# Where the maxima return in an attention quarter, the place of the bias in every second quarter, and the products that release banks first

## The chip, the cores and the metric

The kernel runs on one core of one Trainium2 chip. The metric is the device time of one execution in microseconds (us). Before the change three runs took 632.68, 632.74 and 633.77 us (median 632.74 us). Engine names are those of the profile: PE (matrix products; PEld is its weight load), DVE (vector engine), ACT (scalar engine), POOL and SP (here mostly the issue of DMAs).

## The reference

The program is one layer of a hybrid block: 1024 latent tokens of width 1024 (a grid of 16 rows by 64 columns), 256 context tokens, one input projection, neighbourhood attention with 8 heads of 64 beside a gated short convolution, and one output projection, all in float32. The change lies in the attention:

```python
def neighbourhood_attention(q, k, v, kc, vc, rpb):
    ...
    s_lat = jnp.einsum('biqhd,birkhd->bhiqrk', q_rot, k_rows,
                       preferred_element_type=jnp.float32) * scale + bias
    s_lat = jnp.where(col_valid[:, None, :], s_lat, -jnp.inf)
    s_ctx = jnp.einsum('biqhd,blhd->bhiql', q_plain, kc,
                       preferred_element_type=jnp.float32) * scale
    ...
    p = jax.nn.softmax(s, axis=-1).astype(v.dtype)
    ...
    o = (jnp.einsum('bhiqrk,birkhd->biqhd', p_lat, v_rows)
         + jnp.einsum('bhiql,blhd->biqhd', p_ctx, vc))
```

The convolution branch appears as `bg * centred_short_conv(cg * u) * silu(zc)`; its last product reads a bank of PSUM (the memory into which PE writes its products).

## The kernel before

Every float32 operand is split into a high and a low part, and a product is three products (high by high, high by low, low by high). In the first 262 us the tokens are normalised and projected and keys, queries and values are stored; then comes the attention; from 539 us on the output projection.

The attention is a loop of 35 **quarters**, `quarter(n)`, four to a head. Quarter `n` does parts of several quarters' work: it makes the scores of quarter `n` and the context scores of `n + 1`; it makes the exponentials of `e = n - 2`; and it multiplies the weights of `o = n - 3` by the values. During a quarter PE also runs `TICKS[n]` **ticks** (`next(fill)`), six products each of 128x512, of the projections that attention does not need yet: the attention gate `z`, then for three conv groups the columns u, cg, z and bg. Each such unit (`unit`) fills two banks of PSUM, one half after the other, under the name `pu`; there are two such banks, so the first half of the next unit can start only when the first half of the last one has been read.

While attention runs, the order on PE, ACT, DVE and POOL is that in which the code calls them (`strict`), and each engine waits at the instruction at its head. The order in quarter `n`:

1. `maxima(e)`: two transposes on PE of the running maxima `mx` into a bank `pmx`, and on DVE the reduction `rm` over them. It returns `back`: two transposes on PE of the spread `rm` into the same bank, and the copy `mg` on ACT.
2. On DVE the low part `pll` that is left over from the quarter before (`lat_rest`).
3. `ctx_out(o)`, where `o` is odd: six products `po` of the context's weights `phc`, `plc` and the values.
4. `do_dves(3)`: waiting work of DVE, at most three pieces besides the `soon` queue. Pieces of the `slow` queue with a third entry are those that release a bank `pu`: `times` of the columns bg, the product `cv<-pu,cv`. Then a step of `gating`, if there is one.
5. Where `o` is odd and live (`early`; these are the even quarters 4 to 34): `back()`.
6. `scores`: four products into `pss`. `ctx_scores`: four products into `pc` and their copy `sc` on ACT.
7. Where not `early`: `back()`.
8. For `e`: on DVE the difference `sc<-sc,mg`, on ACT two exponentials (`phc` and `sc`); on DVE the difference `sb<-sb,mg`, on ACT two exponentials (`phl` and `sb`).
9. One tick, then `lat_out(o)`: products `po` of `phl`, `pll`.
10. On DVE the bias, `sb<-pss,bt` (one instruction or two), then the running maxima: `mx<-pc,sc` and two `mx<-mx,sb`. The next quarter's `maxima` needs the last of them.
11. On DVE `plc<-sc,phc`. The remaining ticks; `finish`, which copies a finished bank to `ob`; `do_acts`, waiting work of ACT.

So in an odd quarter PE makes the transposes back after the context's four scores, and in an even one between the context's six products and the scores. In every quarter the bias stands behind the two differences on DVE.

Of the kernel before, what the change touches and what calls it, by code (L numbers as in the profile page):

```python
# [14 lines left out]
ALU = mybir.AluOpType  # L15
# [10 lines left out]
NB = 8  # L26
# [13 lines left out]
def body(tc, es, x, ctxt, w_ada, b_ada, w_in, q_g, k_g, rpbr, w_out, vecs, cst, out):  # L40
# [21 lines left out]
    pe, act, dve, pool = every = [ordered(e) for e in (nc.tensor, nc.scalar, nc.vector, nc.gpsimd)]  # L62
# [258 lines left out]
    def do_acts():  # L321
        for c in soon + (slow if not any(c[1] and c[1].__name__ == "product" for c in soon) else []):
            if c[0]:
                c[0]()
                c[0] = None

    def do_dves(most=99):
        while most > 0 and slow and slow[0][2] is not None and not slow[0][0]:
            slow.pop(0)[1]()
            most -= 1  # L330
        for queue in chores:
            while queue and not queue[0][0] and (queue is soon or most > 0 and not soon):
                on_dve = queue.pop(0)[1]
                if on_dve:
                    on_dve()
                    most -= 1
# [205 lines left out]
    def tr():  # L542
        return ps0.tile([P, 512], F32, name="tr", tag="tr", bufs=2)
# [48 lines left out]
    pv = tr()  # L592
# [243 lines left out]
    for m in range(1, 4):  # L836
        k, new, last = 2 * m, m < 3, m == 3
# [169 lines left out]
    class head:  # L1007
# [28 lines left out]
            self.bt = bmp.tile([P, 3, 384], F32, name="bt", tag="bt", bufs=2)  # L1036
            sp.dma_start(self.bt[:].rearrange("p v n -> p (v n)")[:, :1128], t4_d[self.h])

        def ctx_scores(self, g):
            pc = psm.tile([P, 2, 256], F32, name="pc", tag="C", bufs=2)  # L1040
            q = self.q[:, 1, g * 256:(g + 1) * 256]
            for i in range(2):
                for l in range(2):
                    pe.matmul(pc[:, i], self.kc[:, l, i * P:(i + 1) * P], q,
                              start=(i == 0 and l == 0), stop=(i == 1 and l == 1), skip_group_check=True)
            sc = ap.tile([P, 2, 256], F32, name="sc", tag="sc", bufs=4)
            act.copy(sc, pc)
            self.cps[g] = sc, pc
# [12 lines left out]
            m = seen(mx[:], j)  # L1061
            dve.tensor_tensor(m, m, cells(sb, j), ALU.max)

        def pv(self, bank, cols, j, ph, pl, last):
            first = bank not in self.po
            if first:
                self.po[bank] = psm.tile([P, 512], F32, name="po", tag="O", bufs=2)
            o_ = cols(self.po[bank][0:HD + 1])
            vh, vl = self.v[:, 0, j], self.v[:, 1, j]
            pe.matmul(o_, vh, ph, start=first, stop=False, skip_group_check=True)  # L1070
            pe.matmul(o_, vl, ph, start=False, stop=False, skip_group_check=True)
            pe.matmul(o_, vh, pl, start=False, stop=last, skip_group_check=True)

# [17 lines left out]
            del self.cps[g]  # L1091
            return lambda: dve.tensor_tensor(pl, sc, ph.bitcast(F32), ALU.subtract)

        def ctx_out(self, g):
            if g % 2:
                ph, pl = self.cx
                for i in range(2):
                    self.pv(g // 2, lambda o: o, NB + i, ph[:, i], pl[:, i], False)

        def finish(self, bank):  # L1100

# [5 lines left out]
    def pair_of(n):  # L1107

        h, g = divmod(n, 4)
        return [(a, heads[h], 2 * g + a) for a in range(2)] if 0 <= h < NH else []  # L1110

    def both(v, n, part=slice(0, 31)):

        lo, hi = span(2 * (n % 4))
        return v[:, :, part.start * 12:min(part.stop, hi - lo) * 12]

    def maxima_of(n):

        lo, hi = span(2 * (n % 4))
        v = mg[:]  # L1120
        return bass.AP(v.tensor, v.offset + lo * 16, [list(v.ap)[0], [4, 2], [16, hi - lo], [1, 12]])

    def turned(n):

        g = n % 4
        return [b for b, there in (((2 * g + 2) % NB, n + 1 < 4 * NH), (2 * g + 1, n >= 0)) if there][::-1 if g < 3 else 1]

    def maxima(e):

        blocks = turned(e) if e < 4 * NH else []  # L1130
        nb = len(blocks)
        if not blocks:
            return None
        pm = psm.tile([P, 512], F32, name="pmx", tag="C", bufs=2)
        for i, b in enumerate(blocks):
            pe.transpose(pm[:, i * P:(i + 1) * P], mx[:, b * P:(b + 1) * P], ident)
        rm = ap.tile([P, 2], F32, name="rm", tag="rm", bufs=8)
        dve.tensor_reduce(rm[:, :nb], pm[:, :nb * P].rearrange("p (i k) -> p i k", i=nb), AX.X, ALU.max)

        def back():  # L1140
            for i in range(nb):
                pe.transpose(pm[:, 256 + i * P:256 + (i + 1) * P], rm[:, i:i + 1].broadcast_to([P, P]), ident)
            v, step = mg[:, blocks[0] * P:], (blocks[-1] - blocks[0]) * P or P
            act.copy(bass.AP(v.tensor, v.offset, [list(v.ap)[0], [step, nb], [1, P]]),
                     pm[:, 256:256 + nb * P].rearrange("p (i k) -> p i k", i=nb))
        return back

    def quarter(n):

        live = lambda m: 0 <= m < 4 * NH
        ticks = TICKS[n]
        e, o = n - 2, n - 3
        back = maxima(e) if e >= 0 else None
        while lat_rest:
            lat_rest.pop()()
        if live(o):
            heads[o // 4].ctx_out(o % 4)  # L1160
        do_dves(3)
        if gating and next(gating[0], "end"):
            gating.pop(0)
        early = live(o) and o % 2
        if back and early:
            back()
        now = pair_of(n)
        for i, hd_, j in now:
            hd_.scores(j, sbank[:, i])
        if n == 0:  # L1170
            next(fill)
            ticks -= 1
        ctx_now = [m for m in ([0, 1] if n == 0 else [n + 1]) if live(m)]
        for m in ctx_now:
            heads[m // 4].ctx_scores(m % 4)
        if back and not early:
            back()
        if live(e):
            ctx_rest = heads[e // 4].ctx_exp(e % 4)
            sb = sbs.pop(e)  # L1180
            w = both(sb, e)
            w4 = w.rearrange("p a (c r) -> p a c r", r=12)
            dve.tensor_tensor(w4, w4, maxima_of(e), ALU.subtract)
            exps[e] = [ap.tile([P, 2, 384], F32R, name=m, tag=m, bufs=b) for m, b in (("phl", 2), ("pll", 1))]
            ph, pl = (both(v, e) for v in exps[e])
            act.activation(ph, w, AF.Exp)
            act.activation(w, w, AF.Exp)
        for _ in range(n > 0):
            next(fill, None)
        done = []  # L1190
        if o >= 0:
            pho, plo = exps.pop(o)
            for i, hd_, j in pair_of(o):
                hd_.lat_out(j, pho[:, i], plo[:, i])
                if j in (5, 7):
                    done.append((hd_, j // 7))
                    if j == 7 and hd_.s:
                        ready.append(hd_.p)
        if now:
            sb = sbs[n] = sb_new()  # L1200
            bt = now[0][1].bt[:].rearrange("p v n -> p (v n)")[:, :1128].rearrange("p (a n) -> p a n", a=2)
            for at, slot, w_ in (((0, 31, 8), (8, 15, 16)), ((0, 0, 31),), ((0, 0, 31),), ((0, 0, 15), (15, 39, 8)))[n % 4]:
                dve.tensor_tensor(sb[:, :, at * 12:(at + w_) * 12], sbank[:, :, at * 12:(at + w_) * 12],
                                  bt[:, :, slot * 12:(slot + w_) * 12], ALU.add)
            for m in ctx_now:
                heads[m // 4].ctx_max(m % 4)
            for i, hd_, j in now:
                hd_.lat_max(j, sb[:, i])
        back = maxima(-1) if n == 1 else None
        if live(e):  # L1210
            ctx_rest()
            lat_rest.append(lambda: dve.tensor_tensor(pl, w, ph.bitcast(F32), ALU.subtract))
            if n + 1 >= len(TICKS) or TICKS[n + 1] == 2:
                lat_rest.pop()()
        for _ in range(ticks - (n > 0)):
            next(fill, None)
        if back:
            back()
        for hd_, bank_ in done:
            hd_.finish(bank_)  # L1220
        do_acts()

    heads = [head(h) for h in range(NH)]
    sbs, exps, ready, lat_rest = {}, {}, [], []
# [12 lines left out]
    fill = fillers()  # L1237
# [20 lines left out]
    for n in range(NT + 3):  # L1258


        p, t = divmod(n, NB)
        at = 2 if p < NPAIR - 1 else 0
# [50 lines left out]
        if 1 < n <= NT + 1:  # L1313
            m, r = n - 2, (n - 2) % NB
# [69 lines left out]
    with sbuf("att") as ap, psum("psb") as psb:  # L1384
        sbank = psb.tile([P, 2, 512], F32, name="pss")
        strict[:] = every
        mx = ap.tile([P, T], F32, name="mx")
        sb_new = lambda: ap.tile([P, 2, 384], F32, name="sb", tag="sb", bufs=3)
        mg = ap.tile([P, T], F32, name="mg")
        heads[0].load_v()  # L1390
        for n in range(len(TICKS)):
            h, g = divmod(n, 4)
# [7 lines left out]
            if ready:  # L1400
                p = ready.pop()
# [150 lines left out]
```

## Time and profile before

| what | us |
|---|---|
| median of three runs | 632.74 |
| the profiled execution, its own time | 632.55 |
| its span, first to last instruction | 630.8 |

A view of the stages gives these busy times on the engines (the granted PE clock was 1.00 in all of them):

| stretch of the span | length | PE | PEld | DVE | ACT |
|---|---|---|---|---|---|
| 0 to 262, projections | 262.00 | 259.51 | 227.78 | 176.95 | 139.83 |
| 262 to 521, attention | 259.00 | 255.26 | 212.68 | 211.51 | 160.23 |
| 521 to 539.4, last units | 18.40 | 18.40 | 15.35 | 10.03 | 9.91 |
| 539.4 to the end, output projection | 91.40 | 88.54 | 74.41 | 35.48 | 16.05 |

A row of the timeline reads: start in us from the start of the span, length in us, engine, line, operation, what it writes `<-` what it reads, the shape, how many were merged, and in brackets how long the engine had been idle before it and what the profile takes to have ended that. All work that a helper issues carries line 55, so the names tell what is what. The ends of products on PE are modelled and overlap the next product's start; a distance between two starts says more of PE than a length.

### The profile page before, as it was taken

What the parts mean: (1) busy time and instruction counts of PE and PEld (TensorE: products, weight loads), DVE (VectorE), ACT (ScalarE), POOL (GpSimd) and SP (SyncE); (2) the same over time, 40 slices, a digit from 0 to 9 for tenths busy, and PEclk for the clock granted to TensorE, in tenths of its full rate; (3) what the DMA queues carried; (4) which work ended last, traced back from release to release, by engine and by line L of the source; (5) the groups of instructions that cost most, each with busy time, mean ns of one, the idle gap of its engine ahead of it and who ended that gap; (6) DMA issues with size and microseconds to landing.
All of it is one profiled execution on the core that took longest, in us unless ns stands there. A gap on an engine that the chain in (4) does not pass through costs nothing.

```text
span 630.8 us, 9829 instructions
## 1 busy us (share of the span) xinstructions
PE 621.7 (99%) x3392; PEld 530.2 (84%) x3392; DVE 434.0 (69%) x889; ACT 326.0 (52%) x712; POOL 77.8 (12%) x102
## 2 busy tenths in 40 slices
PE   8999999999999999999999999999999999999998
PEld 3577899999999999888888888788878778888887
DVE  1887858766857755478787888988997855594111
ACT  4776935425526446346576568567674845450000
POOL 1305014123223222000000000000000002003200
PEclk9999999999999999999999999999999999999999
DMA  8983638866875994966555471857442235963631
GB/s 320 366 284 107 180 121 284 270 203 216 273 247 179 291 332 136 341 227 221 158 206 185 155 239 58 275 190 248 133 129 67 60 91 150 362 232 117 217 100 51
DMA packets 104030, 126.45 MB, mean 200 GB/s; under 512 B 10689, under 2 KB 70553, under 8 KB 102700
## 3 DMA queue, kind: packets, MB, share of 16 engines
q1 hardware_dynamic: 97516, 114.24, 54.9%
q10 hardware_dynamic: 6208, 11.05, 5.4%
q0 software_dynamic: 256, 0.54, 0.3%
q8 instruction: 27, 0.44, 0.3%
q14 instruction: 23, 0.19, 0.1%
HBM read 89.04 MB, written 39.04 MB: 203 GB/s over the span
## 4 chain that ended last, share of the span: by engine, by line
PE 91%; DVE 4%; ACT 3%; issue 1%; POOL 0%; ACTq 0%; DVEq 0%; POOLq 0%
PE pu L55 26%; PE pacc L55 21%; PE po L55 7%; PE acc L55 6%; PE pout L75 5%; PE pout L76 5%; PE pout L74 5%; PE tr L55 5%; PE cacc L55 4%; PE pss L55 2%; PE pmx L55 2%; PE pc L55 2%; PE trA L55 1%; PE trB L55 1%; DVE sc L55 1%
## 5 line engine op out<-in xcount | busy, mean ns | idle before, releaser
L55 PE MATMUL pu<-h,uh 128*128 128x512 f32 x544 | 171.3, 396 | 1.4 <-DVE cv L55 1.2
L55 PE MATMUL pacc<-w,h 128*128 128x384 f32 x768 | 138.4, 337 | 0.0
L55 PEld LDWEIGHTS pacc<-w,h 128*128 128x128 f32 x768 | 132.7, 188 | 0.2
L55 PEld LDWEIGHTS pu<-h,uh 128*128 128x128 f32 x544 | 97.6, 188 | 18.9 <-DVE cv L55 1.7
L55 PE MATMUL pu<-h,ul 128*128 128x512 f32 x272 | 106.6, 392 | 0.0
L55 PEld LDWEIGHTS pu<-h,ul 128*128 128x128 f32 x272 | 51.1, 188 | 11.3
L55 POOL TENSOR_TENSOR ss<-ss,few 128x4 f32<-128x4 f32 (+1 forms) x40 | 41.9, 1049 | 124.8 <-DVE ss L55 124.8
L75 PE MATMUL pout<-wol,yh 128*128 128x512 f32 (+2 forms) x136 | 51.6, 379 | 0.0
L74 PE MATMUL pout<-woh,yh 128*128 128x512 f32 (+2 forms) x136 | 51.5, 379 | 0.0
L76 PE MATMUL pout<-woh,yl 128*128 128x512 f32 (+2 forms) x136 | 50.8, 379 | 0.0
L55 PE MATMUL acc<-h,w 128*128 128x512 f32 x144 | 38.1, 405 | 0.8 <-ACT h L55 0.8
L55 ACT COPY sc<-pc 128x512 f32<-128x512 f32 x32 | 18.7, 588 | 36.4 <-PE pc L55 31.2
L55 ACT ACTIVATE sq<-pacc 128x256 f32<-128x256 f32 x32 | 12.4, 387 | 48.0 <-PE pacc L55 47.5
L55 DVE TENSOR_REDUCE rm<-pmx 128x2 f32<-128x256 f32 (+1 forms) x33 | 13.7, 416 | 28.5 <-PE pmx L55 28.3
L55 DVE TENSOR_TENSOR mx<-mx,sb 128x372 f32<-128x372 f32 (+2 forms) x64 | 31.9, 498 | 2.0
L55 PE MATMUL po<-phl,v 128*65 128x276 f32 (+2 forms) x192 | 32.0, 269 | 0.0
L55 ACT ACTIVATE phc<-sc 128x512 fp32r<-128x512 f32 x32 | 20.3, 634 | 22.6 <-DVE sc L55 22.5
L55 DVE TENSOR_REDUCE ss<-sq 128x4 f32<-128x260 f32 (+1 forms) x40 | 15.7, 392 | 23.3 <-ACT sq L55 23.3
L55 ACT ACTIVATE qn<-pacc,ss 128x64 f32<-128x64 f32 x128 | 30.1, 333 | 3.0 <-POOL ss L55 3.0
L55 PEld LDWEIGHTS acc<-h,w 128*128 128x128 f32 x144 | 25.5, 188 | 6.5 <-ACT h L55 1.2
L1482 DVE TENSOR_TENSOR ot<-pout,xr 128x512 f32<-128x512 f32 (+2 forms) x9 | 5.7, 632 | 35.1 <-PE pout L76 33.1
L74 PEld LDWEIGHTS pout<-woh,yh 128*128 128x128 f32 x136 | 25.6, 188 | 4.7
(159 smaller groups left out, 1164.8 us busy)
## 6 DMA issues: line engine op xcount, KB each, us to landing
uraw<-in_w_in SPq DMA_DIRECT2D x34, 256.0 KB
q_d<-qs SPq DMA_DIRECT2D x32, 256.0 KB
k_s<-k_d SPq DMA_DIRECT2D x8, 1024.0 KB
q_s<-q_d SPq DMA_DIRECT2D x16, 512.0 KB
wr<-in_w_in SPq DMA_DIRECT2D x40, 192.0 KB
slab<-in_w_ada SPq DMA_DIRECT2D x6, 1024.0 KB
v_d<-vs SPq DMA_DIRECT2D x20, 260.0 KB
v<-v_d SPq DMA_DIRECT2D x16, 325.0 KB
```

The costliest lines, as they stand in the source:

```text
L55: i = emit(*a, **kw)
L74: i = pe.matmul(ps, ah, bh, start=first, stop=False)
L75: pe.matmul(ps, ah, bl, start=False, stop=False)
L76: pe.matmul(ps, al, bh, start=False, stop=last)
L1482: dve.tensor_tensor(ot[:, c], ps[c.start][:, c], xr[:, c], ALU.add)
```

## The change

Three things change in `quarter`, with two small helpers.

- `back()` is called inside the context's work: in an even quarter after the fourth of the six products of `ctx_out` (ahead of their last two), in an odd one after the second of the four products of `ctx_scores`, and so ahead of the copy `sc` on ACT. Where an odd quarter has no context scores to make, `back()` comes behind the scores as before, except in quarter 33, which has no scores either: one of its ticks is taken ahead of `back()`.
- In the odd quarters from 3 on and in quarter 2 the bias (`biased`) stands ahead of the two differences on DVE; in the even ones it stays where it was.
- `do_frees(1)` puts at most one product that releases a bank ahead of `maxima`, so ahead of the reduction `rm`; the number left for `do_dves` is lowered by it.

```diff
--- before.py
+++ after.py
@@ -324,10 +324,14 @@
                 c[0]()
                 c[0] = None
 
-    def do_dves(most=99):
+    def do_frees(most):
         while most > 0 and slow and slow[0][2] is not None and not slow[0][0]:
             slow.pop(0)[1]()
             most -= 1
+        return most
+
+    def do_dves(most=99):
+        most = do_frees(most)
         for queue in chores:
             while queue and not queue[0][0] and (queue is soon or most > 0 and not soon):
                 on_dve = queue.pop(0)[1]
@@ -1036,10 +1040,12 @@
             self.bt = bmp.tile([P, 3, 384], F32, name="bt", tag="bt", bufs=2)
             sp.dma_start(self.bt[:].rearrange("p v n -> p (v n)")[:, :1128], t4_d[self.h])
 
-        def ctx_scores(self, g):
+        def ctx_scores(self, g, between=None):
             pc = psm.tile([P, 2, 256], F32, name="pc", tag="C", bufs=2)
             q = self.q[:, 1, g * 256:(g + 1) * 256]
             for i in range(2):
+                if i and between:
+                    between()
                 for l in range(2):
                     pe.matmul(pc[:, i], self.kc[:, l, i * P:(i + 1) * P], q,
                               start=(i == 0 and l == 0), stop=(i == 1 and l == 1), skip_group_check=True)
@@ -1061,13 +1067,15 @@
             m = seen(mx[:], j)
             dve.tensor_tensor(m, m, cells(sb, j), ALU.max)
 
-        def pv(self, bank, cols, j, ph, pl, last):
+        def pv(self, bank, cols, j, ph, pl, last, between=None):
             first = bank not in self.po
             if first:
                 self.po[bank] = psm.tile([P, 512], F32, name="po", tag="O", bufs=2)
             o_ = cols(self.po[bank][0:HD + 1])
             vh, vl = self.v[:, 0, j], self.v[:, 1, j]
             pe.matmul(o_, vh, ph, start=first, stop=False, skip_group_check=True)
+            if between:
+                between()
             pe.matmul(o_, vl, ph, start=False, stop=False, skip_group_check=True)
             pe.matmul(o_, vh, pl, start=False, stop=last, skip_group_check=True)
 
@@ -1091,11 +1099,10 @@
             del self.cps[g]
             return lambda: dve.tensor_tensor(pl, sc, ph.bitcast(F32), ALU.subtract)
 
-        def ctx_out(self, g):
-            if g % 2:
-                ph, pl = self.cx
-                for i in range(2):
-                    self.pv(g // 2, lambda o: o, NB + i, ph[:, i], pl[:, i], False)
+        def ctx_out(self, g, between):
+            ph, pl = self.cx
+            for i in range(2):
+                self.pv(g // 2, lambda o: o, NB + i, ph[:, i], pl[:, i], False, between if i else None)
 
         def finish(self, bank):
 
@@ -1153,17 +1160,16 @@
         live = lambda m: 0 <= m < 4 * NH
         ticks = TICKS[n]
         e, o = n - 2, n - 3
+        left = do_frees(1) + 2 if n > 2 else 3
         back = maxima(e) if e >= 0 else None
         while lat_rest:
             lat_rest.pop()()
-        if live(o):
-            heads[o // 4].ctx_out(o % 4)
-        do_dves(3)
+        early = live(o) and o % 2
+        if early:
+            heads[o // 4].ctx_out(o % 4, back)
+        do_dves(left)
         if gating and next(gating[0], "end"):
             gating.pop(0)
-        early = live(o) and o % 2
-        if back and early:
-            back()
         now = pair_of(n)
         for i, hd_, j in now:
             hd_.scores(j, sbank[:, i])
@@ -1172,9 +1178,21 @@
             ticks -= 1
         ctx_now = [m for m in ([0, 1] if n == 0 else [n + 1]) if live(m)]
         for m in ctx_now:
-            heads[m // 4].ctx_scores(m % 4)
-        if back and not early:
+            heads[m // 4].ctx_scores(m % 4, back if n >= 2 and not early else None)
+        if back and not early and not ctx_now:
+            if not now:
+                next(fill, None)
+                ticks -= 1
             back()
+        def biased():
+            sb = sbs[n] = sb_new()
+            bt = now[0][1].bt[:].rearrange("p v n -> p (v n)")[:, :1128].rearrange("p (a n) -> p a n", a=2)
+            for at, slot, w_ in (((0, 31, 8), (8, 15, 16)), ((0, 0, 31),), ((0, 0, 31),), ((0, 0, 15), (15, 39, 8)))[n % 4]:
+                dve.tensor_tensor(sb[:, :, at * 12:(at + w_) * 12], sbank[:, :, at * 12:(at + w_) * 12],
+                                  bt[:, :, slot * 12:(slot + w_) * 12], ALU.add)
+
+        if now and not (early or n < 2):
+            biased()
         if live(e):
             ctx_rest = heads[e // 4].ctx_exp(e % 4)
             sb = sbs.pop(e)
@@ -1197,15 +1215,12 @@
                     if j == 7 and hd_.s:
                         ready.append(hd_.p)
         if now:
-            sb = sbs[n] = sb_new()
-            bt = now[0][1].bt[:].rearrange("p v n -> p (v n)")[:, :1128].rearrange("p (a n) -> p a n", a=2)
-            for at, slot, w_ in (((0, 31, 8), (8, 15, 16)), ((0, 0, 31),), ((0, 0, 31),), ((0, 0, 15), (15, 39, 8)))[n % 4]:
-                dve.tensor_tensor(sb[:, :, at * 12:(at + w_) * 12], sbank[:, :, at * 12:(at + w_) * 12],
-                                  bt[:, :, slot * 12:(slot + w_) * 12], ALU.add)
+            if early or n < 2:
+                biased()
             for m in ctx_now:
                 heads[m // 4].ctx_max(m % 4)
             for i, hd_, j in now:
-                hd_.lat_max(j, sb[:, i])
+                hd_.lat_max(j, sbs[n][:, i])
         back = maxima(-1) if n == 1 else None
         if live(e):
             ctx_rest()
```

## The prediction

> **What bounds the kernel now.** I read the page first, then the waits, then the timeline of PE through the attention.
>
> ```profile
> span 630.8 us, 9829 instructions
> ...
> PE 621.7 (99%) x3392; PEld 530.2 (84%) x3392; DVE 434.0 (69%) x889; ACT 326.0 (52%) x712; POOL 77.8 (12%) x102
> ...
> PE 91%; DVE 4%; ACT 3%; issue 1%; POOL 0%; ACTq 0%; DVEq 0%; POOLq 0%
> ```
>
> PE is busy throughout and the change removes no product. All it can win is time in which PE waits, and the chain shows where that is: 7% of it runs over DVE and ACT. The view of waits names a few, such as this one, a bank `pu` that DVE has not read yet:
>
> ```profile
> PEld pu L55 <- DVE cv L55: 1.7, 2, 0.8
> ```
>
> The idle times in brackets are short because a product's end is modelled, so I measure by starts: a product of 512 columns starts 0.23 us after the one before it, and the first product behind two transposes starts 0.14 after the pair.
>
> ```profile
> 289.11 0.38 PE L55 MATMUL pmx<-ci,mx 128*128 128x128 f32 x2
> ...
> 289.25 0.71 PE L55 MATMUL po<-phc,v 128*65 128x512 f32 x2
> 289.53 0.42 DVE L55 TENSOR_REDUCE rm<-pmx 128x2 f32<-128x256 f32 x1 [0.45 <-PE pmx L55]
> ...
> 290.02 0.62 PE L55 MATMUL po<-phc,v 128*65 128x512 f32 x2
> ...
> 290.71 0.39 PE L55 MATMUL pmx<-ci,rm 128*128 128x128 f32 x2
> ```
>
> This is the head of an even quarter, 4, without a wait: two transposes, six products, two transposes back. The last three products start from 290.02 to 290.48, so the return's new place, ahead of the last two, lies at 290.02 + 0.23 = 290.25.
>
> **Part 1, the bias ahead of the differences, and the earlier return, in the odd quarters.** Quarter 2 and the start of 3:
>
> ```profile
> 278.01 0.59 ACT L55 COPY sc<-pc 128x512 f32<-128x512 f32 x1
> 278.50 0.38 ACT L55 COPY mg<-pmx 128x256 f32<-128x256 f32 x1
> ...
> 278.91 0.69 DVE L55 TENSOR_TENSOR sc<-sc,mg 128x512 f32<-128x512 f32 x1 [0.76 <-ACT mg L55]
> ...
> 280.19 0.93 DVE L55 TENSOR_TENSOR sb<-pss,bt 128x744 f32<-128x744 f32 x1
> ...
> 281.48 1.13 DVE L55 TENSOR_TENSOR mx<-mx,sb 128x372 f32<-128x372 f32 x2
> ...
> 281.95 0.39 PE L55 MATMUL pu<-h,ul 128*128 128x512 f32 x1
> ...
> 282.75 0.41 PE L55 MATMUL pmx<-ci,mx 128*128 128x128 f32 x2 [0.41 <-ACT uh L55]
> ```
>
> PE would have been at 281.95 + 0.23 = 282.18 and starts at 282.75: 0.57 lost. The profile names ACT, but the transposes read `mx`, and its last instruction ends at 281.48 + 1.13 = 282.61; PE follows 0.14 later. So DVE is late, and it idled 0.76 for the maxima `mg`. The bias needs only the scores, which PE made before the context scores whose copy began at 278.01. Placed first, it starts where the idle time began (278.91 - 0.76 = 278.15) and fills it. The copy `mg` meanwhile comes earlier: its transposes skip two context scores, and on ACT it no longer stands behind `sc` (0.49 from start to start). The last `mx` then ends at 281.85, PE could follow at 281.99, before it arrives: **0.57 won**. Bounds: 0 if another input of DVE is late, and 0.57.
>
> Quarter 5 to 6:
>
> ```profile
> 299.73 0.69 DVE L55 TENSOR_TENSOR sc<-sc,mg 128x512 f32<-128x512 f32 x1 [0.42 <-ACT mg L55]
> ...
> 302.57 0.40 PE L55 MATMUL pu<-h,ul 128*128 128x512 f32 x1
> ...
> 303.54 0.41 PE L55 MATMUL pmx<-ci,mx 128*128 128x128 f32 x2 [0.58 <-ACT ob L55]
> ```
>
> Lost: 0.97 - 0.23 = 0.74. DVE idled only 0.42, so **0.42 is won**, 0.32 stays. Later, quarters feed more work to DVE:
>
> ```profile
> 448.77 0.69 DVE L55 TENSOR_TENSOR sc<-sc,mg 128x512 f32<-128x512 f32 x1
> ...
> 452.58 0.41 PE L55 MATMUL pmx<-ci,mx 128*128 128x128 f32 x2 [0.28 <-ACT ob L55]
> ...
> 497.48 0.68 DVE L55 TENSOR_TENSOR sc<-sc,mg 128x512 f32<-128x512 f32 x1
> ...
> 500.82 0.41 PE L55 MATMUL pmx<-ci,mx 128*128 128x128 f32 x2 [0.60 <-DVE mx L55]
> ```
>
> No idle time stands before `sc` there. Another order of the same instructions ends at the same time, so the 0.28 at 452.58 stays. At 500.82 the chain runs through ACT, which makes silus ahead of `mg`; the earlier return in the even quarter 30 lets ACT start its exponentials up to two products (0.46) sooner. Between 0 and 0.60 I take **0.30**, the middle.
>
> What the bias pushes back is the exponentials, by up to 0.93. Two readers follow, `plc` and next quarter's `pll`:
>
> ```profile
> 450.16 0.63 ACT L55 ACTIVATE sc<-sc 128x512 f32<-128x512 f32 x1
> ...
> 452.36 0.68 DVE L55 TENSOR_TENSOR plc<-sc,phc 128x512 fp32r<-128x512 f32 x1
> ```
>
> The second exponential ends at 450.79, 1.57 before `plc` needs it; 0.64 is left. The cover is the running maxima on DVE; cost 0. Without it `plc` and the next `rm` behind it would be late.
>
> **Part 2, products that free banks first.** Quarter 19, then 29:
>
> ```profile
> 401.03 0.42 DVE L55 TENSOR_REDUCE rm<-pmx 128x2 f32<-128x256 f32 x1 [0.84 <-PE pmx L55]
> ...
> 401.81 0.38 PE L55 MATMUL pmx<-ci,rm 128*128 128x128 f32 x2
> ...
> 402.04 1.28 DVE L55 TENSOR_TENSOR cv<-pu,cv 128x512 f32<-128x512 f32 x2
> ...
> 402.78 0.73 PE L55 MATMUL pu<-h,uh 128*128 128x512 f32 x2 [0.58 <-DVE cv L55]
> ...
> 478.85 0.42 DVE L55 TENSOR_REDUCE rm<-pmx 128x2 f32<-128x256 f32 x1 [2.33 <-PE pmx L55]
> ...
> 479.80 0.38 PE L55 MATMUL pmx<-ci,rm 128*128 128x128 f32 x2
> ...
> 480.77 0.73 PE L55 MATMUL pu<-h,uh 128*128 128x512 f32 x2 [0.59 <-DVE cv L55]
> ```
>
> Each time PE starts 0.97 behind its transposes instead of 0.14: 0.83 lost, until the first of two products `cv<-pu,cv` (0.64 each) has read the bank. That product now comes ahead of `rm`, where DVE idles 0.84 and 2.33: in quarter 19 it runs from 400.19 to about 400.83, before `rm` can start at 401.03. **Won: 2 x 0.83 = 1.66.** Bounds: if the cover were gone, `rm` would be 0.64 late and most of it lost again; the two idle times exclude that. Its store to DRAM on SP's queue goes earlier too; only the output projection reads it. DVE's later work in these quarters shrinks by 0.64, so PE, arriving 0.83 sooner, finds `mx` nearly as ready as now. The third conv group's products come after the loop's last reductions and gain nothing.
>
> **Part 3, a tick ahead of the return in quarter 33.**
>
> ```profile
> 510.68 0.27 PE L55 MATMUL pmx<-ci,mx 128*128 128x128 f32 x1
> ...
> 511.34 0.32 PE L55 MATMUL pmx<-ci,rm 128*128 128x128 f32 x1 [0.39 <-DVE rm L55]
> ```
>
> PE stands for 0.66 - 0.14 = 0.52 with nothing to do; a tick, six products (1.38), covers it, if their weights are there, as they were for the products on both sides of the wait. The tick is taken from a later place: **0.52 won**.
>
> **Part 4, does the return come too early?** PE now waits for `rm` sooner, with the rest of the context's products and all else of PE queued behind it. Without cover, PE needs this distance from the first transposes to the return (quarter 31):
>
> ```profile
> 493.98 0.38 PE L55 MATMUL pmx<-ci,mx 128*128 128x128 f32 x2
> ...
> 494.88 0.43 PE L55 MATMUL pmx<-ci,rm 128*128 128x128 f32 x2
> ```
>
> 0.90. In an even quarter the distance becomes 290.25 - 289.11 = 1.14: 0.24 to spare. In odd quarters it shrinks by two scores of 256 columns, 0.23: at its tightest (282.75 to 283.98 before) to 1.00, 0.10 to spare.
>
> ```profile
> 283.98 0.38 PE L55 MATMUL pmx<-ci,rm 128*128 128x128 f32 x2
> ```
>
> Where `rm` starts 0.42 behind the transposes, as at 289.53, that suffices; it does not where DVE comes late with the work ahead of `rm`. The trace has no transposes between the halves of such a group; the bounds are 0 (no product goes away, so there is nothing to gain) and the 0.24 of margin lost again in each of some 30 places, 7 us. Nearest are the rows of quarters 4 and 31, whose margins say 0; I take **-0.2** in all. The Trainium skill, TensorE: Matmul & The Clock Gate, section "Step-by-step: what each phase is for", says that PE pulls only weight loads ahead, one behind the running product. `rm` is such a weight, so by that rule it is wanted one load earlier than the rows of PE say, and the eight tightest quarters would each lose some 0.1, an estimate from the margins above: 0.8 instead of 0.2, and 630.0 us. No row of before shows a return in the new place, so the trace can't settle it yet.
>
> **The sum:** 0.57 + 0.42 + 0.30 + 1.66 + 0.52 - 0.2 = 3.3. The profiled execution took 632.55 us, span and 1.8 around it; less 3.3 is 629.3. The runs' median of 632.74 is 0.2 above that execution, so for them I say **629.4 us**.
>
> **The rivals.** *Vector keeps its pace* (0.15): only what does not hang on DVE's order is won, parts 2 and 3: 2.18 - 0.2, 630.6. For it: 452.58, where order cannot help; against: the brackets of 0.76 and 0.42. *The end takes it back* (0.10):
>
> ```profile
> 569.90 0.69 DVE L1457 TENSOR_TENSOR yl<-tb,yh 128x512 fp32r<-128x512 f32 x1
> ...
> 571.94 1.13 PE pout L76 x5
> ```
>
> The last operand of the output projection is ready at 570.59 and PE takes it within 1.4. If that chain through DRAM does not come earlier with PE, only about 1.4 is kept, 631.2, or less if the compiler orders this end anew, up to 632.5. Against: PE runs into the output projection without a wait now, and the chain's first link is the copy of the attention's last products, which moves with PE. *Slower* (0.10): the exponentials, up to 0.93 later in the odd quarters, meet other work on ACT and pass the remaining 0.64; `plc`, then `rm`, then PE's transposes back are late. From there on each of the 15 odd quarters from 3 to 31 can cost what PE lost at 282.75, 0.41 by the bracket: 6.2 - 3.3 = 2.9 more, 635.4. Against it: the 1.57 above, in a quarter in which DVE was already full; for it: ACT's silus and copies of weights, which stand in the same queue. *It does not do what it says* (0.05): each wait removed is met again at the next product that needs DVE, 632.6; for it speaks that DVE is the engine behind nearly every wait shown, against it that its idle brackets lie just ahead of them.
>
> **How the numbers follow.** My forecast, 628.4 to 630.4, has 0.60. With the first rival it makes 0.75 for faster by over 0.2% (1.27 us, what a measurement of this kernel can tell), below 631.5; the end and "no effect" make 0.15 for within it, the exponentials 0.10 for slower. The range goes down to 628.0, where the 0.32 and 0.28 left over go too, and up to 631.9, most of the way through the end's case: about 0.8.
>
> **What would show it.** Right: `pu` without a wait at quarters 19 and 29, the bias starting where DVE idled before `sc`, no wait at the transposes of quarters 3 and 33, a shorter one at 6. Wrong: PE waiting for `rm` in many quarters (part 4), waits of `plc` for ACT, or idle PE in the output projection.

## The result and the profile after

| | before | after |
|---|---|---|
| median of nine runs, us | 632.95 (632.68 to 634.50) | 629.33 (628.76 to 632.36) |
| ratio, 95% interval | | 0.9947 [0.9931, 0.9963] |
| the profiled execution, own time | 632.55 | 631.49 |
| its span | 630.8 | 629.7 |

Between the medians lie 3.62 us. By the ratio the gain is 0.5%, and the weaker end of its interval, 0.9963, is still a gain of 0.37%, above the 0.2% that the forecast took as the least that can be told. The profiled execution of after is 2.16 above its own median, and its span is only 1.1 shorter than that of before. So its span is not the place to read the gain. Its page:

```profile
PE 621.4 (99%) x3391; PEld 530.9 (84%) x3392; DVE 433.5 (69%) x889; ACT 325.5 (52%) x712; POOL 78.0 (12%) x102
...
PE 88%; DMA 5%; ACT 3%; DVE 2%; issue 1%; ACTq 1%; SPq 1%; DVEq 0%
```

PE is as busy as before. In the chain that ends last DVE has fallen from 4% to 2%, and a share of 5% for DMA is new. To separate the two, the span is cut into stages. The view of one tile gives the first and the last start of its instructions; here are the transposes of `mx` (from the end of quarter 1 to quarter 33) and the third product of the output projection, of before and then of after:

```profile
L55 PE MATMUL pmx<-ci,mx x64: 270/272/306, 273.5 to 510.7; 128*128 128x128 f32 x64
...
L76 PE MATMUL pout<-woh,yl x136: 273/389/390, 539.8 to 627.7; 128*128 128x512 f32 x120, 128*128 128x384 f32 x8, 128*128 128x128 f32 x8
```

```profile
L55 PE MATMUL pmx<-ci,mx x64: 269/272/301, 274.4 to 508.6; 128*128 128x128 f32 x64
...
L76 PE MATMUL pout<-woh,yl x136: 273/389/497, 537.2 to 626.6; 128*128 128x512 f32 x120, 128*128 128x384 f32 x8, 128*128 128x128 f32 x8
```

The loop took 237.2 before and 234.2 after. It began 0.9 later after, behind code that the change doesn't touch, and the output projection took 89.4 where it had taken 87.9. In that projection PE stood once for ACT, which stood for a transfer (the profile names that of `tb`; the cast itself reads `woraw`):

```profile
549.52 1.66 ACT L1448 CAST woh<-woraw 128x512 fp32r<-128x512 f32 x3 [5.80 <-DMA tb<-y_d]
...
552.82 0.39 PE L76 MATMUL pout<-woh,yl 128*128 128x512 f32 x1
554.24 0.50 PE L74 MATMUL pout<-woh,yh 128*128 128x512 f32 x1 [1.03 <-ACT yh L1471]
```

From 552.82 to 554.24 is 1.42 for a step that else takes 0.23. It is met again in one of the eleven experiments' profiles, e4, which does not have the early return; the other ten, and before, have 87.9 to 88.3 there. ACT stands ahead of this cast in all thirteen profiles, 4.24 to 5.25 in eleven of them (4.36 in before) and 5.80 and 5.92 in after and e4; only there does PE wait for it. So it is not bound to the change as a whole. One execution of each kernel was profiled; of after's nine runs seven lie between 628.76 and 629.65, one is this one, 631.49, and what made the last, 632.36, is not known.

In the loop, the rows that answer to those of quarters 2 to 3, 6 and 19 (DVE and PE, timeline):

```profile
278.96 0.93 DVE L55 TENSOR_TENSOR sb<-pss,bt 128x744 f32<-128x744 f32 x1
279.80 0.68 DVE L55 TENSOR_TENSOR sc<-sc,mg 128x512 f32<-128x512 f32 x1
...
282.81 0.39 PE L55 MATMUL pu<-h,ul 128*128 128x512 f32 x1
283.04 0.38 PE L55 MATMUL pmx<-ci,mx 128*128 128x128 f32 x2
...
302.82 0.39 PE L55 MATMUL pu<-h,ul 128*128 128x512 f32 x1
303.33 0.41 PE L55 MATMUL pmx<-ci,mx 128*128 128x128 f32 x2
...
400.01 0.68 DVE L55 TENSOR_TENSOR cv<-pu,cv 128x512 f32<-128x512 f32 x1
400.92 0.42 DVE L55 TENSOR_REDUCE rm<-pmx 128x2 f32<-128x256 f32 x1 [0.22 <-PE pmx L55]
...
401.60 0.48 PE L55 MATMUL pc<-q_s,kc_s 128*128 128x256 f32 x2
401.91 0.63 PE L55 MATMUL pu<-h,uh 128*128 128x512 f32 x2
```

At 278.96 the bias stands where DVE had idled 0.76, and `sc` follows without a bracket. PE takes the transposes of quarter 3 at 283.04, 0.23 behind the product ahead of them: the loss of 0.57 is gone. At 303.33 it is 0.51 behind instead of 0.97. In quarter 19 the first product `cv<-pu,cv`, which releases the bank, now runs ahead of `rm`, and `pu` follows the first of two context scores by 0.31, as it does in quarter 7, which never had this wait (0.32): the wait of 0.83 is gone. Quarter 29 reads the same.

### The profile page after: what moved, and what is told of

It is laid out like the page before. It is cut to its first block, busy times and chain, and to the rows that moved or that the text cites. A ratio compares the mean times of both kernels' runs of the same rounds, so it can differ in the third digit from the quotient of the medians.

```text
span 629.7 us, 9816 instructions
## 1 busy us (share of the span) xinstructions
PE 621.4 (99%) x3391; PEld 530.9 (84%) x3392; DVE 433.5 (69%) x889; ACT 325.5 (52%) x712; POOL 78.0 (12%) x102
## 4 chain that ended last, share of the span: by engine, by line
PE 88%; DMA 5%; ACT 3%; DVE 2%; issue 1%; ACTq 1%; SPq 1%; DVEq 0%
PE pu L55 25%; PE pacc L55 21%; PE po L55 8%; PE acc L55 6%; PE pout L76 4%; PE pout L74 4%; PE pout L75 4%; PE tr L55 4%; PE cacc L55 4%; PE pss L55 3%; DMA woraw<-in_w_out 2%; PE pc L55 2%; PE pmx L55 2%; DMA xx<-in_x 2%; DMA xr<-in_x 1%; PE trA L55 1%
## 5 line engine op out<-in xcount | busy, mean ns | idle before, releaser
L55 ACT COPY mg<-pmx 128x256 f32<-128x256 f32 (+1 forms) x33 | 12.0, 365 | 39.1 <-PE pmx L55 33.9
L76 PEld LDWEIGHTS pout<-woh,yl 128*128 128x128 f32 x136 | 25.6, 188 | 5.1 <-DVE yl L1472 0.4
```

The costliest lines, as they stand in the source:

```text
L55: i = emit(*a, **kw)
L76: pe.matmul(ps, al, bh, start=False, stop=last)
```

## The experiments

Kernels are compared by the runs' ratio to before and, finer, by the **loop**: the time from the start of quarter 2's transposes to that of quarter 33's, from the timeline (the rows above begin at the end of quarter 1, 3 us earlier). Each ratio is to runs of before that were taken with that kernel's (medians 632.77 to 633.04). The ratios' intervals are too wide to tell most of these kernels from one another, so the loop decides between the theories. It is read from one execution of each kernel, but it repeats closely: e4, whose edit lies behind the loop, has 234.31 beside 234.24, and no quarter of it differs by more than 0.03. The **length of a quarter** is the time from the start of its transposes to the start of the next quarter's, so a wait at quarter 3's transposes is in the length of quarter 2. From quarter 33's transposes to the last product `po` it is 10.85 to 10.86 in kernels without the tick ahead of the return, and 10.26 to 10.29 in those with it.

| kernel | what it is | median, us | ratio to before [95%] | loop, us |
|---|---|---|---|---|
| before | | 632.95 | | 234.24 |
| after | | 629.33 | 0.9947 [0.9931, 0.9963] | 231.30 |
| e1_frees | before, bank-freeing product first | 631.56 | 0.9975 [0.9966, 0.9984] | 232.60 |
| e2_bias | before, bias ahead | 632.08 | 0.9990 [0.9979, 1.0001] | 232.86 |
| e3_return | before, early return | 631.41 | 0.9976 [0.9965, 0.9986] | 233.04 |
| e4_tick33 | before, tick in quarter 33 | 632.62 | 0.9988 [0.9979, 0.9998] | 234.31 |
| e5_no_bias | after, bias behind | 629.55 | 0.9949 [0.9937, 0.9961] | 231.31 |
| e6_no_return | after, return in its old places | 629.42 | 0.9952 [0.9939, 0.9964] | 231.26 |
| e7_ticks | after, two ticks moved | 628.45 | 0.9936 [0.9923, 0.9949] | 230.52 |
| e8_ticks_no_bias | e7, bias behind | 628.56 | 0.9933 [0.9921, 0.9945] | 230.36 |
| e9_q7 | after, bias behind in quarter 7 | 628.93 | 0.9941 [0.9920, 0.9961] | 231.17 |
| e10_best | e8, tick in quarter 31 too | 628.32 | 0.9933 [0.9917, 0.9949] | 230.16 |
| e11_earlier | after, return one step earlier | 632.04 | 0.9985 [0.9973, 0.9997] | 233.40 |

**One part alone (e1 to e4).**

```diff
+        left = do_frees(1) + 2 if n > 2 else 3
         back = maxima(e) if e >= 0 else None
...
-        do_dves(3)
+        do_dves(left)
```

> Before, with do_frees(1) ahead of the maxima as the only edit. Theory (each part removes its own waits of PE): the product cv<-pu,cv runs in DVE's idle time ahead of rm, PE no longer waits for pu in quarters 19 and 29, 2 x 0.83 us less: about 631.2 us beside 632.9 of before; all other waits of PE stay as they are. Rival (waits move on): PE arrives sooner at the next transposes and waits there for mx, 632.5 to 632.9.

Measured: 234.24 - 232.60 = 1.64 in the loop; the forecast's part 2 had 1.66. The quarters behind the two, 20 and 30, keep their lengths within 0.02, so the waits do not move on.

```diff
+        if now and not (early or n < 2):
+            biased()
         if live(e):
...
         if now:
+            if early or n < 2:
+                biased()
```

> Before, with the bias ahead of the differences in quarter 2 and the odd quarters as the only edit. Theory (it fills DVE's idle time ahead of sc): the waits at quarters 3 and 6 shrink by 0.57 and 0.42, the others stay, about 631.9 us. Rival (later exponentials cost as much): plc or pll wait for ACT, rm is late in some quarters, 632.5 to 633.

Measured: 1.38, where 0.99 was expected. Quarters 2 and 5 are shorter by 0.57 and 0.51; quarter 31, from which nothing was expected, by 0.12; 13 and 21 by 0.08 and 0.07. The runs alone would not show this: the ratio's interval includes 1. In the PE timeline of this kernel quarter 3 has no wait left:

```profile
282.68 0.39 PE L55 MATMUL pu<-h,ul 128*128 128x512 f32 x1
282.92 0.38 PE L55 MATMUL pmx<-ci,mx 128*128 128x128 f32 x2
```

```diff
-            heads[o // 4].ctx_out(o % 4)
+            heads[o // 4].ctx_out(o % 4, back)
...
-            heads[m // 4].ctx_scores(m % 4)
-        if back and not early:
+            heads[m // 4].ctx_scores(m % 4, back if n >= 2 and not early else None)
+        if back and not early and not ctx_now:
             back()
```

> Before, with only the return of the maxima amid the context's products or scores; bias, do_dves and quarter 33 as before. Theory: mg comes up to 0.7 earlier in odd quarters, so it takes away the same idle time of DVE (0.76 and 0.42) that the bias would fill: waits at 3 and 6 shrink by about 0.5 and 0.4, about 632.0 us, as much as the bias alone. Rival A (the return itself does nothing, the bias is what helps): 632.7 to 632.9. Rival B (PE waits for rm in the new places, 0.1 to 0.24 a quarter): 634 or more.

Measured: 1.20. Quarters 2 and 5 are shorter by 0.51 and 0.50, and no quarter is longer by more than 0.07, so PE does not lose in the new places. At quarter 32's transposes the two edits part. Here is PE with the bias alone (e2), then with the return alone (e3); before had 0.60 in the bracket:

```profile
500.16 0.41 PE L55 MATMUL pmx<-ci,mx 128*128 128x128 f32 x2 [0.48 <-DVE mx L55]
```

```profile
498.79 0.41 PE L55 MATMUL pmx<-ci,mx 128*128 128x128 f32 x2 [0.61 <-DVE mx L55]
```

The return wins nothing there; the bias wins 0.12, although DVE has no idle time ahead of `sc`. DVE in before, then in e2, shows from where:

```profile
498.92 0.79 DVE L55 TENSOR_TENSOR sb<-pss,bt 128x360 f32<-128x360 f32 x2
499.74 0.93 DVE L55 TENSOR_TENSOR mx<-mx,sb 128x276 f32<-128x276 f32 x2
```

```profile
496.95 0.79 DVE L55 TENSOR_TENSOR sb<-pss,bt 128x360 f32<-128x360 f32 x2
497.65 0.68 DVE L55 TENSOR_TENSOR sc<-sc,mg 128x512 f32<-128x512 f32 x1
```

In before `mx` reads the bias's result and starts 0.82 after the bias does; in e2 `sc`, which does not read it, starts 0.70 after. Quarter 31 makes no context scores, so there the bias and the maxima that read it stand side by side unless the bias is moved.

```diff
         if back and not early:
+            if not ctx_now and not now:
+                next(fill, None)
+                ticks -= 1
             back()
```

> Before, with only the tick of quarter 33 taken ahead of the return. Theory: 0.52 us less, about 632.4 us. Rival: the tick is missing later, 632.9 us.

Measured: the loop as before (234.31), and behind it 10.86 became 10.29: 0.57. Its profile is the other one in which the output projection waited, 540.1 to 629.8 by the row of `yl`, 89.7; the median, 632.62, does not carry that.

The four alone add up to 1.64 + 1.38 + 1.20 + 0.57 = 4.79. The whole change has 2.94 in the loop and 0.60 behind it, 3.54, which is 1.25 less. By the lengths of quarters 0.48 in quarter 2 and 0.50 in quarter 5 are counted twice, for the bias and for the return; some 0.2 in 13 and 21 too; and almost 0.2 is lost in quarter 8, where none of the four loses more than 0.03 alone. The next two take the bias or the return from the whole.

**One part missing (e5, e6).**

```diff
-        if now and not (early or n < 2):
-            biased()
...
         if now:
-            if early or n < 2:
-                biased()
+            biased()
```

> The changed kernel with the bias behind the differences again in all quarters. Theory (return and bias take away the same idle time of DVE): about 629.3 us, as the changed kernel; the wait of PE at rm in quarter 8 (0.2 us) and the later exponentials go. Rival (the bias wins the 1.0 us of quarters 3 and 6): 630.3 us, with waits back at the transposes of quarters 3 and 6.

```diff
-            heads[o // 4].ctx_out(o % 4, back)
+            heads[o // 4].ctx_out(o % 4, None)
...
+        if back and early:
+            back()
...
-            heads[m // 4].ctx_scores(m % 4, back if n >= 2 and not early else None)
-        if back and not early and not ctx_now:
+            heads[m // 4].ctx_scores(m % 4, None)
+        if back and not early:
```

> The changed kernel with the return of the maxima in its old places (behind the context's six products or four scores); bias ahead, do_frees and the tick of quarter 33 stay. Theory (the same idle time again): about 629.5 us, waits at 3 and 6 as in the changed kernel. Rival (the return is what wins in quarters 3, 6 and 32): 630.3 us or more.

Measured: 231.31 and 231.26, where the whole has 231.30. In the sum neither is missed. Without the bias (e5) quarters 2 and 31 are longer by 0.08 and 0.11, and quarter 8 is shorter by 0.22; without the early return (e6) quarter 8 is shorter by 0.19. DVE in quarter 2, first without the bias ahead (e5), then without the early return (e6):

```profile
278.61 0.69 DVE L55 TENSOR_TENSOR sc<-sc,mg 128x512 f32<-128x512 f32 x1 [0.25 <-ACT mg L55]
```

```profile
277.95 0.93 DVE L55 TENSOR_TENSOR sb<-pss,bt 128x744 f32<-128x744 f32 x1
278.80 0.69 DVE L55 TENSOR_TENSOR sc<-sc,mg 128x512 f32<-128x512 f32 x1
```

The bracket that was 0.76 before is 0.25 with an early return alone: `mg` comes sooner. With the bias alone `mg` comes as late as ever, but DVE has something to do. In quarters 2 and 5 they are two cures of one wait.

**What is lost in quarter 8 (e9).** The whole change has one wait that neither before nor e5 has. DVE and PE of after:

```profile
317.50 0.93 DVE L55 TENSOR_TENSOR pll<-sb,phl 128x744 fp32r<-128x744 f32 x1 [0.32 <-ACT sb L55]
318.35 0.42 DVE L55 TENSOR_REDUCE rm<-pmx 128x2 f32<-128x256 f32 x1
...
317.55 0.38 PE L55 MATMUL pmx<-ci,mx 128*128 128x128 f32 x2
...
318.47 0.39 PE L55 MATMUL po<-phc,v 128*65 128x512 f32 x1
318.82 0.43 PE L55 MATMUL pmx<-ci,rm 128*128 128x128 f32 x2
```

In quarter 7 the bias pushed the exponentials back, `pll` waits 0.32 for the last of them, `rm` behind it on DVE starts 0.80 after the transposes instead of some 0.42, and PE reaches the return 0.35 after the product ahead of it instead of 0.23. That is 0.12; the product behind the return starts another 0.05 late (0.19 behind it instead of 0.14), 0.17 in all. One quarter's order tells whether that is the cause:

```diff
-        if now and not (early or n < 2):
+        late = early or n < 2 or n == 7
+        if now and not late:
             biased()
...
-            if early or n < 2:
+            if late:
                 biased()
```

> The changed kernel with the bias behind the differences in quarter 7 alone. Theory (in quarter 7, which takes pll into itself because quarter 8 has two ticks, the later exponentials hold DVE at pll, so rm of quarter 8 is late): the 0.2 us that PE waits there go, all else stays; the attention's stretch 0.2 shorter, about 629.1 us. Rival (PE waits there because the return comes too early): the wait stays.

PE and DVE of e9 at that place:

```profile
316.38 0.39 PE L55 MATMUL pmx<-ci,mx 128*128 128x128 f32 x2
...
317.29 0.40 PE L55 MATMUL po<-phc,v 128*65 128x512 f32 x1
317.52 0.38 PE L55 MATMUL pmx<-ci,rm 128*128 128x128 f32 x2
...
316.80 0.42 DVE L55 TENSOR_REDUCE rm<-pmx 128x2 f32<-128x256 f32 x1
```

`rm` starts 0.42 after the transposes and the wait is gone; quarter 8 is 0.20 shorter, the loop 0.13. In e6 the same wait of `pll` stands on DVE, but the return lies behind all six products, 1.59 after the transposes, and PE loses nothing:

```profile
316.53 0.93 DVE L55 TENSOR_TENSOR pll<-sb,phl 128x744 fp32r<-128x744 f32 x1 [0.33 <-ACT sb L55]
...
316.56 0.39 PE L55 MATMUL pmx<-ci,mx 128*128 128x128 f32 x2
...
318.15 0.38 PE L55 MATMUL pmx<-ci,rm 128*128 128x128 f32 x2
```

So it takes both edits to lose in this quarter: the bias makes `rm` late, and the early return takes away the cover.

**How much room the return has (e11).** The return moved one step further, ahead of the fourth of the context's six products and ahead of all four context scores:

```diff
-                if i and between:
+                if not i and between:
                     between()
...
-            pe.matmul(o_, vh, ph, start=first, stop=False, skip_group_check=True)
             if between:
                 between()
+            pe.matmul(o_, vh, ph, start=first, stop=False, skip_group_check=True)
```

> The changed kernel with the return one step earlier still: ahead of the fourth of the context's six products, and ahead of all four context scores. Theory (PE needs 0.90 us from the first transposes to the return): distances fall to 0.91 in even quarters, 0.90 in quarters 5, 9 and so on, 0.74 in 3, 7 and so on; only the last lose, 7 x 0.16 = 1.1 us, about 630.4 us. Rival (weights are wanted one load earlier): every place loses 0.1 to 0.2, some 30 places, 632.5 to 634 us.

Measured: the loop is 2.10 longer than after's, where 1.1 was expected; the median, 632.04, lies between the theory's 630.4 and the rival's 632.5. Quarter 7 in after (PE and its weight loads), then in e11 (also DVE):

```profile
311.21 0.38 PE L55 MATMUL pmx<-ci,mx 128*128 128x128 f32 x2
311.34 0.76 PE L55 MATMUL pss<-q_s,k_s 128*128 128x276 f32 x4
311.94 0.40 PE L55 MATMUL pc<-q_s,kc_s 128*128 128x256 f32 x2
312.18 0.38 PE L55 MATMUL pmx<-ci,rm 128*128 128x128 f32 x2
...
312.10 0.21 PEld L55 LDWEIGHTS pmx<-ci,rm 128*128 128x128 f32 x2
```

```profile
310.10 0.38 PE L55 MATMUL pmx<-ci,mx 128*128 128x128 f32 x2
310.23 0.76 PE L55 MATMUL pss<-q_s,k_s 128*128 128x276 f32 x4
310.99 0.43 PE L55 MATMUL pmx<-ci,rm 128*128 128x128 f32 x2
311.18 0.72 PE L55 MATMUL pc<-q_s,kc_s 128*128 128x256 f32 x4
...
310.99 0.19 PEld L55 LDWEIGHTS pmx<-ci,rm 128*128 128x128 f32 x2 [0.23 <-DVE rm L55]
...
310.51 0.42 DVE L55 TENSOR_REDUCE rm<-pmx 128x2 f32<-128x256 f32 x1 [1.69 <-PE pmx L55]
```

The four scores take 0.60 (311.34 to 311.94), so PE of e11 could have gone on at 310.83. `rm` ends at 310.93, its load and the product start at 310.99: 0.16 late, and 0.05 more are lost in the pair. That is 0.21 in a quarter of this kind. Six of the seven, 3 to 23, are longer by 0.20 to 0.25, 1.3 in all, and 27 by nothing. The other 0.8 the theory had at nothing: it is 0.03 to 0.06 in most of the remaining quarters, where the return now stands 0.90 to 0.94 behind the transposes. In after the same return comes 0.97 behind them in quarter 7, with the load 0.08 ahead of the product and nothing lost. Of the places tried, the change has the earliest that is free in these quarters.

**Two ticks moved (e7, e8, e10).** After still loses at two quarters' heads, by starts: 0.51 - 0.23 = 0.28 in quarter 6 and 0.60 in quarter 32 (below). In both, PE arrives at the transposes of `mx` before DVE has finished it. One tick more in the quarter ahead covers that, taken from the next. The edit does a second thing, which its forecast does not name: a quarter in front of one with two ticks makes its own `pll` (`TICKS[n + 1] == 2`), so that of quarter 5 now stands ahead of quarter 6's `rm`.

```diff
-TICKS = [2, 3, 3, 3, 3, 2, 3, 3, 2] + 2 * (8 * [3] + 2 * [4]) + 3 * [3] + [5, 4, 4]
+TICKS = [2, 3, 3, 3, 3, 3, 2, 3, 2] + 2 * (8 * [3] + 2 * [4]) + [3, 3, 4, 4, 4, 4]
```

> The changed kernel with one tick moved from quarter 6 to quarter 5 and one from 32 to 31 (TICKS 3,2 in place of 2,3, and 4,4 in place of 3,5). Theory (what is left at quarters 6 and 32 is DVE's and ACT's own length against PE's): a tick of 1.36 us covers the 0.3 and 0.6 left there, the quarters after have 1.8 and 10 us to spare, about 628.4 us. Rival (the wait comes again one quarter later): 629.3 us.

> The same moved ticks, with the bias behind the differences in all quarters. Theory (bias redundant, and a cost at quarter 8): 628.2 to 628.4 us. Rival (bias needed): 629.3 us.

Quarter 32 in after, then in e7 (PE):

```profile
497.89 0.39 PE L55 MATMUL pu<-h,ul 128*128 128x512 f32 x1
498.72 0.41 PE L55 MATMUL pmx<-ci,mx 128*128 128x128 f32 x2 [0.45 <-DVE mx L55]
```

```profile
498.28 0.39 PE L55 MATMUL pu<-h,ul 128*128 128x512 f32 x1
498.51 0.38 PE L55 MATMUL pmx<-ci,mx 128*128 128x128 f32 x2
```

The step of 0.83 has become 0.23, so all 0.60 is won. The step of 0.51 in quarter 6 has become 0.23 too. Of these 0.88 the loop keeps 0.78. In quarter 6 it loses again what the moved `pll` costs; DVE and PE of e7:

```profile
304.38 0.42 DVE L55 TENSOR_REDUCE rm<-pmx 128x2 f32<-128x256 f32 x1
...
304.85 0.43 PE L55 MATMUL pmx<-ci,rm 128*128 128x128 f32 x2
```

`rm` starts 0.78 behind the transposes at 303.60 (0.44 in after), the return 0.35 behind the product ahead of it, and the product behind the return 0.19 later: 0.17, as in quarter 8. This time it is so without the bias too (e8), so `pll` ahead of `rm` and the early return are enough. With the bias behind everywhere (e8) the loop is 0.16 shorter still: quarter 8 wins 0.23 and quarter 2 loses 0.08. The last one has in addition a tick ahead of the return in quarter 31, which has scores but no context scores to cover it:

```diff
         if back and not early and not ctx_now:
-            if not now:
-                next(fill, None)
-                ticks -= 1
+            next(fill, None)
+            ticks -= 1
             back()
```

> The moved ticks, bias behind everywhere, return amid the products, and a tick ahead of the return in quarter 31 as in 33. Theory (PE waits at quarter 31 only for lack of work between transposes and return): 0.2 us less than with the moved ticks alone, about 628.2 us, faster than both kernels. Rival (the tick only moves the wait to the transposes of quarter 32, since mg and the chain behind it come later): as the moved ticks, 628.5 us.

Measured: 628.32, and a loop of 230.16, 1.14 less than after's. Quarter 31 is 0.16 shorter than in e8 and quarter 32 no longer, so the wait does not move on. This version is faster than before and after by its median. The intervals of its ratio and after's overlap; the difference rests on the loop. Between e7, e8 and e10 the runs can't choose. Without the bias ahead it is also the simpler change.

## Why the prediction was right, point by point

The forecast was 629.4 us and the runs' median is 629.33. Its sum was 3.3; the loop and what follows it show 3.54, and the medians of nine runs 3.62. That the numbers lie this close is in part luck: the median of before moved by 0.21 from the three runs that the forecast had to the nine, one term was too large by 0.15, and the others together too small by 0.4.

- **The bias and the return in the odd quarters.** Quarter 3 went as forecast. In quarter 6, 0.46 was won from start to start (0.42 forecast) and the rest stayed, as forecast, and so did the wait of quarter 26 (PE of after, the answer to the row at 452.58):

```profile
451.47 0.41 PE L55 MATMUL pmx<-ci,mx 128*128 128x128 f32 x2 [0.28 <-DVE mx L55]
```

  The term of **0.30 for quarter 32 was mis-sized, and its reason was wrong**: by brackets 0.60 became 0.45, 0.15 won. The forecast gave it to the early return of quarter 30, which would let ACT start sooner. With the return alone the wait is 0.61 (e3), with the bias alone 0.48 (e2), and `mg` starts 2.76 behind quarter 31's transposes in before and in e3 alike. What was won is the bias's, from which the forecast had expected nothing, since another order of the same instructions would end at the same time: it ends 0.12 sooner where it parts an instruction of DVE from the one that reads its result. A tick ahead of the wait closes it, by e7. This part and part 4 together had 1.09 in the sum; after against e1 has 232.60 - 231.30 = 1.30. By the lengths of quarters 0.60 of it is won in quarter 2, 0.52 in 5, 0.11 in 31, 0.07 each in 21 and 29, and 0.16 is lost in 8; the last 0.1 is spread.
- **What the working did not separate.** It priced the bias and the return as one cure and named what each does, but not that either is enough. Its number holds; as a reason for keeping both edits it does not, by e5 and e6: what the bias wins beside the return, in quarters 2 and 31, is no more than it costs in quarter 8.
- **Products that free banks first.** 1.66 forecast, 1.64 by e1, in the two quarters named, and the cover named (DVE's idle time ahead of `rm`) held: 0.22 is left of it in quarter 19.
- **The tick in quarter 33.** 0.52 forecast, 0.57 measured alone (e4) and 0.60 in the whole change.
- **The return too early.** -0.2 was taken as a little in many places. What was found is 0.17, all in quarter 8, and it takes the bias as well; the return alone (e3) does not lose it. That the size agrees is luck. The margins from quarters 4 and 31 held in the tight ones, where 1.00 was forecast and 0.97 came, since in before quarter 7 and its like have 1.20 and not the 1.23 of quarter 3. The Trainium skill, TensorE: Matmul & The Clock Gate, section "Step-by-step: what each phase is for", has the weight load pulled ahead of the running product, from which 0.8 was estimated as lost. The load indeed starts ahead, at 312.10 for a product at 312.18, but `rm` was ready in time; no tight quarter shows that loss, and these are seven, not eight, since in quarter 31 the return stays behind the scores. The 2.10 of one step earlier does not bear the rule out either: in its tight quarters `rm` itself ends after PE is free (310.93 and 310.83).
- **The rivals.** *Vector keeps its pace* falls with quarter 3, and *it does not do what it says* with the loop. *The end takes it back* looks right in the one profiled execution, 631.49, which shows idle PE in the output projection, a sign that the forecast had named for being wrong. The runs speak against it: the wait came in after and in e4, and not in e5 to e10, which end attention as early as after or earlier. What makes it come was not tried. *Slower* named a real mechanism: exponentials that come too late because of the bias. It came to bear in one quarter, through `pll` and not `plc`, and cost 0.17. The times of three rivals, 630.6, 631.2 and 635.4, were counted from the profiled 632.55 and not, as the forecast, from the median; that moves each by 0.2 and decides nothing.

Open stays what the loop still loses: some 0.4 in quarter 26, 0.5 to 0.7 in quarter 27 and 0.1 to 0.2 in quarter 28, in after as in e5 to e8. No run tried to win them.

## What to carry to other kernels

When two edits shorten the same wait, one from the supply side (the value comes sooner) and one from the demand side (the engine does something else first), price each alone and with the other: their gains don't add, and here keeping both even cost 0.17 in one quarter. Look too at what else a changed number switches, as the ticks did with `pll`. A return trip between engines can be read off one place without cover; here it had the same length wherever nothing covered it, 0.89 to 0.90. Put at least that much work of the first engine between the two ends. And read a gain of half a per cent in the stage that was edited, start to start, because the span of one execution varied by more in stages that nobody touched.

## What the runs showed of the hardware

- **The trip PE to DVE and back is 0.89 to 0.90** from the start of two 128x128 transposes to the first product that uses their reduction: 0.41 until `rm` starts, 0.42 for it, 0.06 until the weight load. At a distance of 0.97 (quarter 7 of after) nothing is lost; where the work between allowed 0.73 (310.10 to 310.83), e11 lost 0.16 and 0.05 behind it.
- **On DVE a reader waits longer for its turn.** In before's loop an instruction that reads what the one ahead of it wrote starts 0.03 to 0.04 after that one's end (the second `mx` behind the first, 30 times; `tb` behind `zs`, 5 times); one that does not starts 0.08 to 0.09 before the end (`plc` behind `mx`, 30 times). That is 0.12 between the two orders, what the bias won in quarter 31.
- **An unchanged stage varied.** The output projection took 89.4 and 89.7 in two profiles and 87.9 to 88.3 in eleven, with ACT idle 5.80 and 5.92 ahead of the cast shown above in the two and 4.24 to 5.25 in the eleven. Why that transfer came late was not tried.
